# The expert stage of a two-block transformer kernel on one core: weights stored by pairs of experts, TensorE's order written out, the loop for overfull experts after the first pair

## The chip, the core and the metric

The kernel runs on one core of one Trainium2 chip. The metric is the device time of one execution in microseconds (us), lower is better. A core has four compute engines that matter here: TensorE (PE in the profile; its weight loads are listed apart as PEld), VectorE (DVE), ScalarE (ACT) and GpSimd (POOL), and SyncE (SP), which issues most of the transfers from memory. [...]

## What is computed

The reference runs a first block (a mixer of differential attention and an mLSTM, cross-attention, a mixture of experts) and then two layers of a second block. All tensors are float32, 512 tokens of 1024 features. The change touches the mixture of experts alone. There are 32 experts of 512 hidden features in 4 groups; each token goes to two of them:

```
def hierarchical_moe(h, w_rg, b_rg, w_re, b_re, w1, w3, w2):
    ...
    top_p, top_i = lax.top_k(jax.nn.softmax(e_logits, axis=-1), TOP_K)
    comb = g_w[:, None] * top_p / jnp.sum(top_p, axis=-1, keepdims=True)
    ...
    def run_block(args):
        x_blk, e = args
        return (jax.nn.silu(x_blk @ w1[e]) * (x_blk @ w3[e])) @ w2[e]
    ...
    out = jnp.zeros((n_tok + 1, d), yb.dtype).at[buf_tok].add(yb)[:n_tok]
    return out.reshape(bsz, seq, d)
```

Every expert's weights are read once: w1 and w3 are 1024 x 512, w2 is 512 x 1024, together 6 MiB per expert and 192 MiB for all.

## The kernel before

**Slots and pairs.** The routing step finds a place for every token in its two experts. An expert has 64 slots (`SLOT`); two experts, `2 * pr` and `2 * pr + 1`, form a pair and share the 128 rows of a tile, so there are 16 pairs. For a pair the stage does the following, each a step by name in `plan` and a function in `experts`:

- `sel`: VectorE makes one-hots `Sel` of tokens by slots.
- `gather`: TensorE multiplies the tokens' rows (in two float16 halves, `hh` and `hl`) by `Sel`, 32 products for each half of the features (`gs`), into a bank named `tr`; VectorE copies the result with a gain to `xg`.
- `w13`: the rows `xg` times w1 and w3, into two banks `h`. The products are float32 and only 64 columns of the array wide, one for each expert of the pair: expert 0 writes the partitions 0 to 63 of a bank, expert 1 the partitions 64 to 127 (`pair`). A float32 product shows as two records in the trace.
- `marks`: four transposes of `Sel` and four small products; ScalarE copies the turned one-hots to `sT`, VectorE reduces the slots' weights to `cw`.
- `hidden`: ScalarE takes a tanh of bank `h`, two VectorE steps make silu(h1) * h3 in `hm`.
- `turn`: four transposes of `hm` into a `tr` bank, ScalarE copies to `hT`.
- `w2` and `y`: `hT` times w2 into two banks `y`, in halves of the output's columns; ScalarE and VectorE split the result into `yh` and `yl`.
- `combine`: for each of 4 tiles of tokens and each half of the columns two products of `sT` with `yh` and `yl` into a `tr` bank, which VectorE adds to `x`. There are two `tr` banks, and `gather`, `marks`, `turn` and `combine` all take turns on them.

**Order.** `plan` sets the order in which the steps are written: `w13` of pair p in four pieces, with `turn`, `w2`, `y` and `combine` of pair p - 1 and the `gather` of pair p + 1 between them. The framework's scheduler then orders each engine's instructions by their dependences and priorities, so TensorE's order need not be the written one.

**Weights.** A piece is 1 MiB, 128 partitions of 2048 float32, and belongs to one expert: four pieces hold w1 and w3, two hold w2. A step of `w13` takes two pieces, one of each expert. There are 19 slots for pieces (`RINGS`); `fetch` writes the loads on SP's queue in the order of use, `piece` writes those up to 15 ahead of the piece that is taken. A load waits on SP until the slot's last user on TensorE is done, and what stands behind it on the queue waits too.

**Overfull experts.** `more` is a loop that runs as often as there are blocks of tokens past the 64 slots. Its count comes from the data; with these inputs the trace has no instruction of its body. Every engine passes the loop's head and they wait for each other there. It stands in pair 4 (`MORE`).

Of the kernel before, what the change touches and what calls it, by code (L numbers as in the profile page):

```python
# [32 lines left out]
MORE = 4  # L33
# [25 lines left out]
def brow(ap):  # L59
    """A row of memory for all partitions."""  # L60
    return bass.AP(tensor=ap.tensor, offset=ap.offset, ap=[[0, P], [1, ap.shape[-1]]])


class Kern:
    def __init__(self, ctx, tc, a):
        self.ctx, self.tc, self.nc, self.a = ctx, tc, tc.nc, a
        self.ssq = {}

    # ---------------------------------------------------------------- pools
# [36 lines left out]
    def split(self, src, hi, lo, scale, ahead=None):  # L106
        """hi + lo = src * scale, each in float16."""
# [6 lines left out]
    def raw_w(self, src, n=2048):  # L114
        """One piece of weights from memory."""
# [4 lines left out]
    def load_w(self, src, n=2048, raw=None):  # L120
        """A piece of weights, split in two halves, by parts of 1024 columns."""
# [11 lines left out]
    def chunk(self, w, c, width):  # L133
        """Chunk c of a piece in halves, a number of columns wide."""
# [3 lines left out]
    def rstd4(self, pool, ss, n, scale):  # L138
        """(ss * scale + EPS) ** -0.5 of a compact [128, n] tile."""
# [7 lines left out]
    def rstd_row(self, pool, src, tag="junk"):  # L147
        """(mean of squares + EPS) ** -0.5 of rows of D, a half at a time."""
# [10 lines left out]
    def bcast_rows(self, pool, r, n, tag):  # L159
        """Row t of every partition = r[t], for n tiles of tokens: [128, n * 128]."""  # L160
# [17 lines left out]
    def grow(self, pool, name):  # L178
        """A gain by features, for all partitions."""
# [4 lines left out]
    def norm_T(self, pool, src, g, xh, xl, i, bank="tr"):  # L184
        """The normalised rows of tile i, by features, in halves."""
# [16 lines left out]
    def raw_steps(self, pool, x, g, xh, xl, r4, i, hf):  # L202
        """A half of the rows of tile i by the gain, by features, in halves; the norm's factor beside it."""
# [8 lines left out]
    def half_rstd(self, pool, x, r4, i, hf, m):  # L212
        """r4[:, i] = m * (mean of squares + EPS) ** -0.5 of the rows, by halves."""
# [10 lines left out]
    def turn_split(self, t, xh, xl, bank="tr", scale=SA):  # L224
        """Four blocks of features of a tile of tokens, turned, in halves."""
# [5 lines left out]
    def consts(self, low):  # L231
# [5 lines left out]
        # the functions' tables are in by the time the rows are  # L237
# [29 lines left out]
    def silu_c(self, pool):  # L267
        """The second block's condition, through its silu, by features, to memory."""
# [8 lines left out]
    def late_consts(self):  # L277
# [3 lines left out]
        # key after query: rows are queries in the one, keys in the other  # L281
# [27 lines left out]
    # ---------------------------------------------------------- first mixer  # L309
    def mixer(self, low, big, pool, early, adp):  # L310
# [28 lines left out]
        # queries and keys of the differential attention, turned  # L339
# [66 lines left out]
    def proj_feat(self, w, xs, width, b, n=S, m=P, out=None, cs=range(DC)):  # L406
        """Columns b*128.. of a piece [d, width] by tokens: [128 features, n tokens]."""
# [8 lines left out]
    def proj_tok(self, w, xs, i, width=256, out=None):  # L416
        """Tokens of tile i by the columns of a piece: [128 tokens, width]."""
# [6 lines left out]
    def turned_head(self, y, yy, c):  # L424
        """One block of features of all tokens, turned, with its gain, in halves."""
# [94 lines left out]
            # root mean square over the head's values  # L520
# [12 lines left out]
    def mlstm(self, pool, xh, xl, qh, ql, gateb, yy):  # L533
# [4 lines left out]
        # gates: logarithms of the forget gates summed up, in rows of tokens  # L538
# [27 lines left out]
        # exp(-m) * SA  # L566
# [3 lines left out]
        # queries and keys: convolution over the tokens, silu  # L570
# [19 lines left out]
        # values with a column of ones, output gates  # L590
# [18 lines left out]
        for h in range(4):  # L609
# [43 lines left out]
            # layer norm over the head  # L653
# [1237 lines left out]
```

## Time and profile before

| | us |
|---|---|
| median of 3 executions | 1729.56 |
| lowest, highest | 1729.55, 1733.49 |
| span of the profiled execution, first to last instruction | 1725.9 |
| expert stage, first to last product with w1 or w3 | 506.2 to 1049.9 |
| tanh of the first pair to tanh of the last (15 pairs) | 522.47 to 1049.66 |

The profile was taken of one execution, for which only the span is listed; the median of the runs is 3.7 us more, which is what lies ahead of the first and behind the last instruction. [...] A DMA share of 1.00 means that all 16 of the core's DMA engines were busy in the stretch. In a row of TensorE's timeline the first number is the start and the second the duration to the end of the last record of the row; the distance between the starts of two rows is the time that TensorE spent on the first, since products are pipelined.

### The profile page before, as it was taken

To read this page: it belongs to the slowest core of one execution; us is meant where nothing else is said; L and a number is where in the kernel's file an instruction comes from. 1 tells how busy PE (TensorE), PEld (TensorE's weight loads), DVE (VectorE), ACT (ScalarE), POOL (GpSimd) and SP (SyncE) were. 2 spreads that over 40 slices of the span, in tenths; PEclk is the share of its full clock that TensorE was granted. 3 is DMA by queue.
4 is the path that set the end of the run, shared out by engine and by line. 5 is a ranking of instruction groups with operands and counts; after the bars stand their busy time and mean duration, and the time that the engine had idled before them with its cause. 6 is when DMAs were issued, how large, how long until landed. Compare 5 with 4: busy or idle time off the path is not lost.

```text
span 1725.9 us, 25286 instructions
## 1 busy us (share of the span) xinstructions
PE 1583.1 (92%) x10208; PEld 832.1 (48%) x10208; DVE 975.8 (57%) x2076; ACT 592.2 (34%) x1230; POOL 113.1 (7%) x124
## 2 busy tenths in 40 slices
PE   7999998989989999999999997798899989888998
PEld 5344676855763333333333332533444674334457
DVE  5779758877562222322232225789465657866462
ACT  5255455323420100011000103732466545227461
POOL 0210001000000000000000002301100012010000
PEclk9999999999999999999999999999999999989999
DMA  7410233995849987999887852133211222340201
GB/s 275 154 53 25 98 111 99 346 293 182 311 183 420 398 328 291 427 399 386 353 339 309 329 220 98 56 99 89 88 49 50 87 68 74 101 125 25 73 26 50
DMA packets 55609, 323.03 MB, mean 187 GB/s; under 512 B 8720, under 2 KB 11584, under 8 KB 19520
## 3 DMA queue, kind: packets, MB, share of 16 engines
q1 hardware_dynamic: 45136, 306.01, 46.8%
q10 hardware_dynamic: 10352, 15.37, 3.4%
q8 instruction: 81, 1.33, 0.3%
q14 instruction: 40, 0.33, 0.1%
HBM read 310.35 MB, written 3.69 MB: 182 GB/s over the span
## 4 chain that ended last, share of the span: by engine, by line
PE 41%; DVE 10%; DMA 4%; ACT 3%; issue 2%; POOL 1%; ACTq 0%; DVEq 0%; POOLq 0%; SPq 0%
PE h L98 10%; PE mm L98 6%; PE cv L98 6%; PE y L98 5%; PE tr L98 5%; PE po L98 4%; PE at L98 3%; DMA R<-cu 3%; DVE sc L1573 1%; DVE m L1572 1%; PE tr L1614 1%; DVE wl L112 1%; DVE sc L1568 1%; DVE yl L112 1%; POOL rs_r L144 1%
## 5 line engine op out<-in xcount | busy, mean ns | idle before, releaser
L98 PE MATMUL h<-raw,xg 128*64 128x512 f32 x1024 | 307.4, 604 | 0.0
L112 DVE SCALAR_TENSOR_TENSOR wl<-raw,wh 128x1024 f16<-128x1024 f32 (+1 forms) x107 | 135.5, 1271 | 63.2 <-ACT wh L111 63.1
L98 PEld LDWEIGHTS <-wh 128*128 128x128 f16 x1104 | 107.5, 100 | 123.4 <-issue 32.3
L98 PEld LDWEIGHTS h<-raw,xg 128*64 128x64 f32 x1024 | 82.4, 137 | 147.1 <-issue 138.8
L98 PE MATMUL y<-raw,hT 128*64 128x512 f32 x512 | 143.7, 595 | 0.7 <-ACT hT L961 0.7
L111 ACT ACTIVATE wh<-raw 128x1024 f16<-128x1024 f32 (+1 forms) x107 | 110.6, 1042 | 91.6 <-PE mm L98 41.8
L112 DVE SCALAR_TENSOR_TENSOR yl<-y,cw,yh 128x512 f16<-128x512 f32 x32 | 24.0, 751 | 190.2 <-ACT yh L111 183.1
L979 DVE SCALAR_TENSOR_TENSOR x<-tr,x 128x512 f32<-128x512 f32 x128 | 84.4, 687 | 46.6 <-PE tr L98 45.4
L111 ACT ACTIVATE yh<-y,cw 128x512 f16<-128x512 f32 x32 | 22.0, 687 | 246.5 <-PE y L98 246.5
L98 PEld LDWEIGHTS <-hh 128*128 128x128 f16 x768 | 73.9, 100 | 35.3 <-issue 30.4
L98 PEld LDWEIGHTS <-wl 128*128 128x128 f16 x552 | 54.9, 100 | 64.0 <-issue 14.5
L98 PEld LDWEIGHTS y<-raw,hT 128*64 128x64 f32 x512 | 42.7, 136 | 69.7 <-issue 67.1
L98 PE MATMUL po<-R,wd 128*32 128x512 f16 x768 | 55.6, 394 | 21.9 <-DMA R<-cu 21.9
L98 PE MATMUL cv<-hl,wh 128*128 128x512 f16 x192 | 74.9, 390 | 0.0
L98 PE MATMUL cv<-hh,wl 128*128 128x512 f16 x192 | 74.9, 390 | 0.0
L98 PE MATMUL cv<-hh,wh 128*128 128x512 f16 x192 | 74.7, 389 | 0.0
L98 PEld LDWEIGHTS <-hl 128*128 128x128 f16 x640 | 64.0, 100 | 4.6 <-issue 2.1
L919 DVE TENSOR_TENSOR xg<-tr,gcol 128x512 f32<-128x512 f32 x30 | 20.7, 692 | 79.5 <-PE tr L98 79.5
L935 ACT ACTIVATE sT<-tr 128x512 f16<-128x512 f16 x16 | 9.6, 597 | 163.2 <-PE tr L933 157.4
L1230 DVE CUSTOM_DVE_ANT_0 raw<-raw,cact 128x1024 f32<-128x1024 f32 x48 | 58.3, 1238 | 10.9 <-DMA raw<-in_w_ada 9.5
L98 PEld LDWEIGHTS <-sT 128*128 128x128 f16 x256 | 20.2, 97 | 89.0 <-issue 75.1
L98 PE MATMUL tr<-yh,sT 128*128 128x512 f16 x128 | 48.8, 384 | 14.6 <-DVE x L979 8.0
(429 smaller groups left out, 3521.3 us busy)
## 6 DMA issues: line engine op xcount, KB each, us to landing
raw<-in_w_moe SPq DMA_DIRECT2D x192, 1024.0 KB, 7.9
raw<-in_w_pre SPq DMA_DIRECT2D x34, 1024.0 KB, 5.7
raw<-in_w_big SPq DMA_DIRECT2D x30, 1024.0 KB, 4.9
raw<-in_w_ada SPq DMA_DIRECT2D x24, 1024.0 KB, 5.2
R<-cu ACTq DMA_DIRECT2D x32, 271.0 KB, 5.0
x<-in_x_tm SPq DMA_DIRECT2D x4, 512.0 KB, 7.3
gt<-in_r ACTq DMA_DIRECT2D x4, 512.0 KB, 5.4
out<-x SPq DMA_DIRECT2D x4, 512.0 KB, 2.6
```

The source lines that it names most:

```text
L98: self.last_mm = self.nc.tensor.matmul(out, lhsT, rhs, start=start, stop=stop, skip_group_check=True)
L111: return (nc.scalar.activation(hi, src, func, scale=scale), nc.vector.scalar_tensor_tensor(lo, src, scale, hi, op0=OP.mult, op1=OP.subtract))
L112: nc.vector.scalar_tensor_tensor(lo, src, scale, hi, op0=OP.mult, op1=OP.subtract))
L144: self.last_pow = nc.gpsimd.tensor_tensor(r[:, :n], t[:, :n], self.mhalf[:, :n], OP.pow)
L919: self.nc.vector.tensor_tensor(xg, pv, self.gcol[:, 4 * g:4 * g + 4, None].to_broadcast([P, 4, P]), OP.mult)
L935: nc.scalar.activation(sT, pt, AF.Copy)
L979: self.last_add = nc.vector.scalar_tensor_tensor(xo, pc, 1.0 / 1024.0, xo, op0=OP.mult, op1=OP.add)
L1230: nc.vector.tensor_tensor_reduce(w, w, cact, 1.0, 0.0, OP.mult, OP.add, to)
L1568: nc.vector.scalar_tensor_tensor(sc, re[:, :W], s, sc, op0=OP.mult, op1=OP.add)
L1572: nc.vector.max(m8, sc)
L1573: nc.vector.match_replace(sc, m8, sc, -3.0e38)
L1614: nc.tensor.transpose(pt[:, (i - k) * P:(i - k + 1) * P], ps_[i][:, k * P:(k + 1) * P], self.ident)
```

## The change

The weights are laid out anew in memory, outside the measured kernel: a piece is still 1 MiB but holds the same part of both experts of a pair. So `w13` of a pair is eight pieces, one for each 128 features, and `w2` is four. `piece` writes loads up to 18 ahead in place of 15.

`plan` writes another order. All of `w13` of a pair comes first, then `hidden` and `marks`, then eight units, each with eight products of the gather of the next pair (`rows`) and one `combine` of the pair before; `turn` stands after the sixth unit (`TURNED`), and `w2` of the same pair follows the units. While the stage is written, `pinned` is set, and every product and transpose goes through `pin`, which has the scheduler keep TensorE's instructions in the written order. The other engines are still ordered by the scheduler.

The gather gets two banks of its own, `ga`; of the four banks `h` two are left. `more` moves behind `w13` of the first pair, ahead of its `hidden`, and uses the banks `y` and `ga`.

```diff
-MORE = 4
+TURNED = 5
...
+        self.pinned = False
...
-        self.last_mm = self.nc.tensor.matmul(out, lhsT, rhs, start=start, stop=stop, skip_group_check=True)
+        self.last_mm = self.pin(self.nc.tensor.matmul(out, lhsT, rhs, start=start, stop=stop, skip_group_check=True))
         return self.last_mm
+    def turned(self, out, src, ident):
+        return self.pin(self.nc.tensor.transpose(out, src, ident))
+    def pin(self, ins):
+        return self.tc.keep_in_program_order(ins) if self.pinned else ins
...
         for p in range(n):
-            was, more = p > 0, p + 1 < n
-            steps += [("w13", p, 0), ("marks", p)]
...
+            more = p + 1 < n
+            if p:
+                steps += [("sel", p + 1)] * more
+            steps += [("w13", p, c) for c in range(DC)]
+            if p == 0:
+                steps += [("more",), ("sel", 1)]
+            steps += [("hidden", p), ("marks", p)]
+            units = [(i, f) for i in range(NT) for f in range(2)]
             if more:
+                steps.append(("open", p + 1))
+            for u, (i, f) in enumerate(units):
+                if more:
+                    steps.append(("rows", p + 1, i, f))
+                if p:
+                    steps.append(("combine", i, (f,)))
+                if u == TURNED:
+                    steps.append(("turn", p))
+            if more:
+                steps += [("close", p + 1)]
+                for k in range(2):
+                    steps += [("w2", p, k, 0), ("w2", p, k, 1), ("y", p, k)]
...
-        self.fetch(k + sum(RINGS) - 4)
+        self.fetch(k + sum(RINGS) - 1)
...
-            raws = [self.piece(2 * pr + j, q).rearrange("p (c f) -> p c f", c=2) for j in range(2)]
-            for cc in range(2):
-                for k in range(2):
-                    for j in range(2):
-                        self.up13(self.ph, k, raws[j][:, cc, k * 512:(k + 1) * 512], xgs[2 * pr + q // 2], 2 * q + cc, pair[j])
+            raw = self.piece(pr, c).rearrange("p (j k f) -> p j k f", j=2, k=2)
+            for k in range(2):
+                for j in range(2):
+                    self.up13(self.ph, k, raw[:, j, k], xgs[2 * pr + c // 4], c, pair[j])
...
+        self.pinned = True
         for st in self.steps:
             do[st[0]](*st[1:])
+        self.pinned = False
...
-            K.banks(c1, "ps2", tr=2, h=4, y=2)
+            K.banks(c1, "ps2", tr=2, ga=2, h=2, y=2)
```

**TensorE, a pair in the stage.** In the names, `h` is a bank of `w13`, `y` one of `w2`, `raw` a piece of weights, `tr<-yh,sT` and `tr<-yl,sT` the two products of a `combine`; the numbers tell tiles apart. Before, in the middle of a pair, with pieces of one expert each:

```order
L98 MATMUL tr_7667<-yl_7579,sT_7319 128x512
L98 MATMUL h_7726<-raw_7432,xg_7615 64x512
L98 MATMUL h_7727<-raw_7430,xg_7615 64x512
L98 LDWEIGHTS sT_7319
L98 MATMUL tr_7671<-yh_7578,sT_7319 128x512
```

Now, at the end of a pair's units, its `w2` and the first `w13` of the next pair:

```order
L99 MATMUL tr_7529<-yl_7339,sT_7204 128x512
L99 MATMUL y_7537<-raw_7165,hT_7507 64x512 x4
L99 MATMUL y_7537<-raw_7171,hT_7507 64x512 x4
L99 MATMUL y_7538<-raw_7177,hT_7507 64x512 x4
L99 MATMUL y_7538<-raw_7183,hT_7507 64x512 x4
L99 MATMUL h_7571<-raw_7189,xg_7533 64x512 x2
L99 MATMUL h_7572<-raw_7189,xg_7533 64x512 x2
```

Where single products with w1 and w3 stood between the products of the combines, all 16 products of `w2` now stand in one run, and the 32 of `w13` in the next, both experts side by side.

**VectorE, a pair in the stage.** `hm` is `hidden`, `cw` belongs to `marks`, `Sel` to `sel`, the steps on `x` are the adds of the combines. Before, where the adds of a pair meet the next `hidden`:

```order
L112 SCALAR_TENSOR_TENSOR yl_8005<-y_7991,cw_7752,yh_8004 128x512
L979 SCALAR_TENSOR_TENSOR x0_82<-tr_8089,x0_82 128x512
L979 SCALAR_TENSOR_TENSOR x1_83<-tr_8093,x1_83 128x512
L950 SCALAR_TENSOR_TENSOR hm_8081<-hm_8081,h_7939 128x512
L979 SCALAR_TENSOR_TENSOR x1_83<-tr_8097,x1_83 128x512
L951 TENSOR_TENSOR hm_8081<-hm_8081,h_7940 128x512
```

Now, from the end of a pair's `w13` on:

```order
L958 SCALAR_TENSOR_TENSOR hm_6769<-hm_6769,h_6719 128x512
L1074 TENSOR_REDUCE cw_6785<-tr_6780 64x1
L959 TENSOR_TENSOR hm_6769<-hm_6769,h_6720 128x512
L1074 TENSOR_REDUCE cw_6785<-tr_6780 64x1
L1062 TENSOR_TENSOR Sel_6930<-slots_4687,pos_5161 128x512
L1075 TENSOR_SCALAR cw_6785<-cw_6785 128x1
L987 SCALAR_TENSOR_TENSOR x0_82<-tr_6799,x0_82 128x512
```

`hidden`, the reductions and the one-hots of a later pair now all stand ahead of the first add of a pair.

**SP, the loads around the loop.** `raw<-in_w_moe` is the load of a piece, `TENSOR_LOAD n_more` and the branch are the loop's head. Before:

```order
L1036 DMA raw<-in_w_moe 128x2048 x66
L1139 TENSOR_LOAD n_more
L1143 COMPARE_AND_BRANCH
L1143 UNCONDITIONAL_BRANCH x2
L1886 BRANCH_PREFETCH_HINT
```

Now:

```order
L1043 DMA raw<-in_w_moe 128x2048 x21
L1153 TENSOR_LOAD n_more
L1157 COMPARE_AND_BRANCH
L1157 UNCONDITIONAL_BRANCH x2
L1908 BRANCH_PREFETCH_HINT
```

Four loads stand further ahead in both; so 25 of the 192 pieces are now issued before the loop's head, where 70 were. Ahead of the stage and behind it the order of every engine is what it was.

## Rows read from the trace of the kernel before

**Rows 1.** The page: its span, and the chain that ended last by engine.

```profile
span 1725.9 us, 25286 instructions
...
PE 41%; DVE 10%; DMA 4%; ACT 3%; issue 2%; POOL 1%; ACTq 0%; DVEq 0%; POOLq 0%; SPq 0%
```

**Rows 2.** Tile h: one record's ns min/median/max, first and last start in us.

```profile
L98 PE MATMUL h<-raw,xg x1024: 592/592/1116, 506.2 to 1049.9; 128*64 128x512 f32 x171
```

**Rows 3.** ACT's timeline (start, us, what): one tanh for each pair, five of 16.

```profile
691.52 0.60 ACT L949 ACTIVATE hm<-h 128x512 f32<-128x512 f32 x1 [1.86 <-PE h L98]
723.69 0.60 ACT L949 ACTIVATE hm<-h 128x512 f32<-128x512 f32 x1 [1.86 <-PE h L98]
...
976.87 0.60 ACT L949 ACTIVATE hm<-h 128x512 f32<-128x512 f32 x1 [5.13 <-PE h L98]
1014.84 0.60 ACT L949 ACTIVATE hm<-h 128x512 f32<-128x512 f32 x1 [5.13 <-PE h L98]
1049.66 0.60 ACT L949 ACTIVATE hm<-h 128x512 f32<-128x512 f32 x1 [5.13 <-PE h L98]
```

**Rows 4.** Windows of one pair: us, busy by engine, PEclk, DMA share, GB/s.

```profile
764.15:796.30 32.15, 32.15 (x190) 12.25 (x190) 10.49 (x18) 3.17 (x5) 0.00 (x0) 1.00 0.97 391
...
908.10:946.10 38.00, 35.75 (x190) 13.56 (x190) 10.30 (x18) 3.17 (x5) 0.00 (x0) 1.00 0.86 332
```

**Rows 5.** PE's timeline in a pair of 32 us, 736 to 759 us.

```profile
736.68 0.64 PE L958 MATMUL tr<-ident,hm 128*128 128x128 f32 x4
...
744.26 0.23 PE L98 MATMUL tr<-Sel,hh 128*128 128x128 f16 x1
...
746.15 3.65 PE L98 MATMUL h<-raw,xg 128*64 128x512 f32 x16
749.64 3.60 PE L98 MATMUL y<-raw,hT 128*64 128x512 f32 x16
753.07 3.60 PE L98 MATMUL h<-raw,xg 128*64 128x512 f32 x16
756.61 0.39 PE L98 MATMUL tr<-yh,sT 128*128 128x512 f16 x1
...
757.58 1.07 PE L98 MATMUL h<-raw,xg 128*64 128x512 f32 x2
758.58 0.39 PE L98 MATMUL tr<-yh,sT 128*128 128x512 f16 x1
```

**Rows 6.** PE's timeline in a pair of 38 us, 895 to 898 us.

```profile
895.85 0.38 PE L98 MATMUL tr<-yh,sT 128*128 128x512 f16 x1 [0.72 <-ACT yh L111]
...
897.79 0.38 PE L98 MATMUL tr<-yh,sT 128*128 128x512 f16 x1 [0.35 <-DVE x L979]
```

**Rows 7.** All engines' timeline, last pair: a combine, its adds, the start of w2.

```profile
1045.37 0.38 PE L98 MATMUL tr<-yl,sT 128*128 128x512 f16 x1 [0.41 <-DVE yl L112]
...
1045.79 1.29 DVE L979 SCALAR_TENSOR_TENSOR x<-tr,x 128x512 f32<-128x512 f32 x2 [0.47 <-PE tr L98]
...
1046.53 0.38 PE L98 MATMUL tr<-yh,sT 128*128 128x512 f16 x1 [0.35 <-DVE x L979]
...
1055.61 3.65 PE L98 MATMUL y<-raw,hT 128*64 128x512 f32 x16 [0.75 <-ACT hT L961]
```

**Rows 8.** DVE's timeline around the loop's head.

```profile
659.24 3.44 DVE L979 SCALAR_TENSOR_TENSOR x<-tr,x 128x512 f32<-128x512 f32 x5 [3.77 <-PE tr L98]
664.10 0.69 DVE L1055 TENSOR_TENSOR Sel<-slots,pos 128x512 f16<-128x512 f32 x1 [1.42 <-ACT hm L949]
```

**Rows 9.** SP's timeline ahead of the stage: loads of pieces, counted at the end.

```profile
443.54 24.05 SPq L1036 DMA_DIRECT2D raw<-in_w_moe  x10
...
495.68 6.55 SPq L1036 DMA_DIRECT2D raw<-in_w_moe  x5
```

**Rows 10.** Windows: the early stage; and four us behind the loop's head.

```profile
540.00:560.00 20.00, 20.00 (x111) 7.14 (x108) 7.72 (x13) 1.28 (x2) 0.00 (x0) 1.00 1.01 427
...
664.00:668.00 4.00, 4.00 (x36) 3.21 (x36) 2.67 (x4) 0.00 (x0) 0.00 (x0) 0.57 0.89 303
```

More of the change, by code (lines that the diff above doesn't have):

```diff
@@ L986, in plan @@
         steps = [("blocks",)]
-        w2 = lambda p, k: [("w2", p, k, 0), ("w2", p, k, 1), ("y", p, k)]
         for p in range(n):
-            was, more = p > 0, p + 1 < n
-            steps += [("w13", p, 0), ("marks", p)]
-            if more:
-                steps.append(("sel", p + 1))
-            if was:
-                steps.append(("turn", p - 1))
-            steps.append(("w13", p, 1))
-            if was:
-                steps += w2(p - 1, 0)
-            if more:
-                steps.append(("gather", p + 1, (0,)))
-            steps.append(("w13", p, 2))
-            if was:
-                steps += w2(p - 1, 1)
-            steps.append(("w13", p, 3))
-            if p != MORE:
-                steps.append(("hidden", p))
-            if was:
-                steps += [("combine", i, (0, 1)) for i in range(NT)]
-            if p == MORE:
-                steps += [("more",), ("hidden", p)]
-            if more:
-                steps.append(("gather", p + 1, (1,)))
@@ L1013, in plan @@
+        steps += [*w2(0)[:2], ("latent", 0), ("y", n - 1, 0),
                   *[("combine", i, (0,)) for i in range(NT)], ("sums",), ("latent", 1),
-                  *w2(n - 1, 1), *[("combine", i, (1,)) for i in range(NT)]]
+                  *w2(1), *[("combine", i, (1,)) for i in range(NT)]]
         self.steps, self.order = steps, []
@@ L1017, in plan @@
             if st[0] == "w13":
-                self.order += [(2 * st[1] + j, st[2]) for j in range(2)]
-            if st[0] == "w2" and st[3] == 0:
-                self.order += [(2 * st[1] + j, 4 + st[2]) for j in range(2)]
+                self.order.append((st[1], st[2]))
+            if st[0] == "w2":
+                self.order.append((st[1], DC + 2 * st[2] + st[3]))
         self.order[-2:-2] = [(NE, 0), (NE, 1)]
@@ L1033, in fetch @@
             raw = self.rings[k % sum(RINGS)].tile([P, 2048], F32, name="raw", tag="raw")
[L1034 to L1036 removed]
+            pr, q = self.order[k]
+            if pr < NE:
+                self.nc.sync.dma_start(raw, self.a["w_moe"][pr, q])
             else:
@@ L1100, in w2 @@
         def w2(pr, k, half):
-            if half == 0:
-                if k == 0:
-                    self.py = [self.bank("y"), self.bank("y")]
-                self.raws = [self.piece(2 * pr + j, 4 + k).rearrange("p (f o) -> p f o", f=4) for j in range(2)]
-            for f in (2 * half, 2 * half + 1):
+            if k == half == 0:
+                self.py = [self.bank("y"), self.bank("y")]
+            raw = self.piece(pr, DC + 2 * k + half).rearrange("p (j f o) -> p j f o", j=2, f=2)
+            for f in range(2):
+                g = 2 * half + f
                 for j in range(2):
-                    self.mm(self.py[k][pair[j]], hT[pr][:, f, pair[j]], self.raws[j][:, f], f == 0, f == 3)
+                    self.mm(self.py[k][pair[j]], hT[pr][:, g, pair[j]], raw[:, j, f], g == 0, g == 3)
         def y(pr, k):
@@ L1128, in sums @@
                                           accum_out=self.fss[:, i:i + 1])
-        do = dict(sel=sel, gather=gather, marks=mark, w13=w13, hidden=hidden, turn=turn, w2=w2, y=y,
+        do = dict(sel=sel, open=rows_open, rows=rows, close=rows_close, marks=mark, w13=w13, hidden=hidden, turn=turn, w2=w2, y=y,
                   combine=lambda i, f: self.combine(quad[-1], i, halves=f), more=lambda: self.more(pool, moe),
                   blocks=lambda: self.blocks(pool), latent=latent, sums=sums)
+        self.pinned = True
         for st in self.steps:
             do[st[0]](*st[1:])
+        self.pinned = False
     def more(self, pool, moe):
```

57 lines of the change are left out of this document (32 added, 25 removed).

## The prediction

> **What bounds the kernel now.** I read the page first: of the chain that ended last TensorE holds 41% [rows 1]. The only stage that the change touches runs from the first product with w1 or w3 at 506.2 to the start of the last at 1049.9 us [rows 2], which I end at 1050.3; that is 544 of 1725.9 us. Then I asked for the tanh of each pair, since one per pair gives the period [rows 3]. There are two periods: 32.17 us (691.52 to 723.69) and 37.97 us (976.87 to 1014.84). The windows of one pair say what sets them [rows 4]. [...] So TensorE's own sequence is the bound in both, and the stream follows it. A pair is 12.58 MB, which over 32.17 us is the 391 GB/s of the first window: that is TensorE's pace and not the stream's limit, which shows where slots are free: 427 GB/s at a DMA share of 1.01 [rows 10].
>
> The timeline of TensorE shows what the sequence loses. Eight products of w1, w3 or w2 in one run (16 records) take 3.43 to 3.49 us, 0.43 each [rows 5], because the two experts' products run side by side on the two halves of the array. A product that stands alone between combines (two records at 757.58) holds TensorE for 1.00 us until the next starts [rows 5]: its partner is missing, and there is a switch to float16 products (about 0.14: 1.00 less two records at 0.43). In the long pairs there are waits besides, as 0.72 us for `yh` and 0.35 us for an add [rows 6].
>
> **The change, a full pair.** TensorE's work in the new order, each kind by its count and a row [rows 5]: 32 products of w13 at 0.43 are 13.8; 16 of w2, 6.9; the 64 of the gather, two lots of 32 in 1.89 us (744.26 to 746.15), 3.8; the 16 of the combines, four lots of four in 0.97 us (756.61 to 757.58), 3.9; the turn 0.6; marks, eight small records that no row above shows alone, between nothing and the turn's 0.6, and I take 0.6, the nearest row. Together 29.6. The lots of 1.89 and 0.97 hold a switch each, six in all, where the new order switches three times a pair: less 3 x 0.14, so 29.2.
>
> To that come the waits of a fixed order, since TensorE can no longer do something else when a bank is late. Let E be the end of w13. The tanh starts 0.6 us before E [rows 2, 3] and takes 0.60; then ScalarE copies `sT`, of the same size, so until about E + 1.1. VectorE does the two steps of `hidden` and the one-hots, three steps of one size at the 0.69 of the one-hots [rows 8], with the small reductions between, before its first add at about E + 2.5. TensorE wants the bank of `sT` for the first combine at E + 1.1 (marks 0.6, eight products of the gather 0.5), that of the reductions for the second at E + 2.1, and the first add's bank for the third at E + 3.0, where the add (0.65, half of a row of two) ends at 3.15 [rows 7]. From there a unit of TensorE is 0.95 us against an add of 0.65, so TensorE sets the pace. I price this at 0.5 us a pair; it can be 0, and the upper end is the rival below. **Period: 29.7 us.** The other queues have cover: the load of a piece is issued when its slot is free, up to 18 pieces ahead; with two banks `h` in place of four the next w13 comes some 15 us after `hidden` has read them; `w2` waits for `hT`, whose copy runs beside the last two units; `close` (two copies of about 0.69) runs beside w2's 6.9 us. Where one of these covers failed, it would cost its own 0.6 to 1.4 us a pair.
>
> **The first pair and the loop.** w13 runs for 13.8 us. Then all engines meet at the loop. Before, VectorE's last add ended at 662.68 (659.24 + 3.44) and its next step began 1.42 us later [rows 8]. I take 1.4 here, with nothing to wait for but w13's end. Behind it comes `sel`, 0.69, now beside marks; then the gather 3.8, turn 0.6, w2 6.9: 27.2 us in all. On SP only loads stand behind the loop. Piece 25 is the first of them, its slot is the seventh piece's, and TensorE frees that about 2 us before the loop, so the stream has loads in flight across it. A granted clock of 0.57 for some 4 us stood behind the loop before [rows 10], and may again; up to 1.7 us, left to the range.
>
> **The sum.** The last w13 ends at 506.2 + 27.2 + 14 x 29.7 + 13.8 = 963.0, against 1050.3: 87.3 us earlier. The last pair then pays: its eight combines of the pair before now stand behind w13 with no gather between, so VectorE sets it: two steps of `hidden` 1.4, eight adds at 0.65 are 5.2, a copy 0.6, so w2 starts 7.2 us after E, where it started 5.3 us after (1055.61) [rows 7]: 1.9 us lost, between 0 and 3. Behind that the order is unchanged. Span 1725.9 - 85.4 = 1640.5; the median lies 3.7 above the span (1729.56), so **1644 us**.
>
> **Does the stream keep up?** Fifteen loads are issued ahead of the stage [rows 9] after four earlier ones, so all 19 slots are on their way when the first product runs. The first slot comes free at about 508, and 169 more pieces of 1.05 MB are needed up to the end of the last w13. With some 5 us for landing and use, at 427 GB/s (2.46 us a piece) that ends at 928, well before 963; at 391 (2.68) at 966. It decides below about 394 GB/s.
>
> **Rivals.**
> *The stream sets the pace.* If 391 GB/s is its sustained limit after all (its DMA share was 0.97 [rows 4]), the last w13 ends at 966 and the time is 1647. If it were held at the 332 GB/s of the long pairs [rows 4] (3.16 us a piece, 1047) nothing would be gained: 1728. Midway between the two windows, at 361 (2.90 us a piece, 1003), it would be 1684. Against all of it: 427 was reached where slots were free [rows 10], and these two rates are those of TensorE's pace.
> [...]
>
> *Banks one at a time.* If each combine waited for the add of the one before, a combine would take 1.38 us (0.22 for its first product, then 1045.37 to 1046.53) [rows 7], the gather hidden in the wait: 11.0 us for eight in place of 7.7, a period of 33.1, and 1692. For it: turn, marks and combines share two banks. Against: two banks alternate, and the gather's 0.47 lies between.
>
> [...]
>
> That the order is not kept is no rival: the built kernel has it.
>
> **How the numbers follow.** The forecast, TensorE's sequence at 29.7 us: 0.70, 1644 us. The stream at 391: 0.10, 1647. At 361: 0.02, 1684. Banks one at a time: 0.09, 1692. A stream that gains nothing: 0.04, 1728. The clock: 0.05, 1752. For the range: no waits at all (14 x 0.5), no loss at the end and marks at 0.3 bring 1644 down to about 1632; waits of 1.9 us a pair, the clock behind the loop and the stream at 391 bring it to 1670. These two ends leave out the last four cases, 0.20. Faster by over 0.3% (about what a measurement of this kernel can tell from no change): 0.91. Within it: 0.04. Slower: 0.05.
>
> **What would show it.** Right: tanh to tanh 29 to 31 us for fourteen pairs, all alike; w13 as one run of 64 records in 13.8 us; the stream at some 424 GB/s over a pair (12.58 MB in 29.7 us) with no wait of TensorE for a piece; the last product with w1 or w3 near 963. Wrong: TensorE's waits on `raw` (the stream), waits of 0.7 us or more at each combine (banks), a granted clock under 1.00 in the middle of pairs (clock), or a second block that runs longer than before.

## The result and the profile after

The changed kernel takes 1646.86 us (median of 5 runs, 1645.52 to 1654.38), against 1730.62 (5 runs, 1729.55 to 1733.49): a ratio of 0.953, 95% interval 0.951 to 0.955. The forecast was 1644 us, within 1632 to 1670. The sum of the prediction came out 3 us off, but two of its terms missed by more than that, in opposite directions: the loop cost 10.0 us where 1.4 were taken, and each pair took 0.44 us less than forecast, 6.2 us over fourteen.

From the page of the changed kernel, the counterpart of [rows 1]: the span, engine times, and in 40 slices the clock granted to TensorE (a share of full speed, here in tenths) and the stream.

```profile
span 1652.7 us, 25283 instructions
PE 1511.4 (91%) x10208; PEld 828.4 (50%) x10208; DVE 973.2 (59%) x2076; ACT 592.0 (36%) x1230; POOL 113.7 (7%) x124
PEclk9999899999998999999999998989999999989999
GB/s 284 157 62 12 91 82 111 290 255 328 147 224 283 385 426 427 427 426 427 426 426 426 426 154 14 109 105 131 10 68 43 75 96 100 67 121 26 77 26 52
PE 48%; DVE 9%; DMA 3%; ACT 3%; issue 2%; POOL 1%; ACTq 0%; DVEq 0%; POOLq 0%
```

The profiled execution is the slowest of the five. The expert stage begins 5.3 us later in it than before (511.47 against 506.2), although nothing changed ahead of it; in the other profiled executions of this study it begins between 505.35 and 513.48. So times are compared below from the first product with w1 or w3 to the last tanh: 543.5 us before (506.2 to 1049.7), 459.7 after (511.47 to 971.14). That is 83.8 us, the whole difference of the medians. Within this stretch the first run of w13 products takes 14.5 to 16.0 us from one profile to another, since the granted clock is still low at its start (0.58 to 0.79 between 505 and 512 us in four profiles), so a difference of about a microsecond there says nothing.

The tanh of the pairs, the counterpart of [rows 3]: start, duration, what, and in brackets ScalarE's idle time ahead and what ended it.

```profile
534.65 0.60 ACT L957 ACTIVATE hm<-h 128x512 f32<-128x512 f32 x1 [24.38 <-SPq L1157]
561.70 0.60 ACT L957 ACTIVATE hm<-h 128x512 f32<-128x512 f32 x1 [12.19 <-PE h L99]
590.96 0.60 ACT L957 ACTIVATE hm<-h 128x512 f32<-128x512 f32 x1 [12.19 <-PE h L99]
620.22 0.60 ACT L957 ACTIVATE hm<-h 128x512 f32<-128x512 f32 x1 [12.19 <-PE h L99]
649.47 0.60 ACT L957 ACTIVATE hm<-h 128x512 f32<-128x512 f32 x1 [12.19 <-PE h L99]
...
942.07 0.60 ACT L957 ACTIVATE hm<-h 128x512 f32<-128x512 f32 x1 [12.19 <-PE h L99]
971.14 0.60 ACT L957 ACTIVATE hm<-h 128x512 f32<-128x512 f32 x1 [12.19 <-PE h L99]
```

Where [rows 3] had two periods, 32.17 and 37.97, there is one of 29.26 us, every pair alike to 0.02 and the last 0.2 shorter. Only the first row is of another kind: its tanh waited for SyncE at line 1157, the loop.

One full pair, from its tanh to the next: the window (engine busy times with counts, granted clock, DMA share, GB/s), and TensorE's timeline without the gather's products.

```profile
620.22:649.48 29.26, 29.09 (x190) 12.65 (x188) 10.37 (x18) 3.17 (x6) 0.00 (x0) 1.00 1.01 426
```

```profile
620.96 0.40 PE L103 MATMUL tr<-identh,Sel 128*128 128x128 f16 x4
621.19 0.24 PE L99 MATMUL tr<-chl,Sel 128*128 128x4 f16 x4
622.04 0.38 PE L99 MATMUL tr<-yh,sT 128*128 128x512 f16 x1
622.26 0.38 PE L99 MATMUL tr<-yl,sT 128*128 128x512 f16 x1
...
627.12 0.65 PE L103 MATMUL tr<-ident,hm 128*128 128x128 f32 x4
...
629.47 7.09 PE L99 MATMUL y<-raw,hT 128*64 128x512 f32 x32
636.38 13.90 PE L99 MATMUL h<-raw,xg 128*64 128x512 f32 x64
```

TensorE is busy for 29.09 of 29.26 us at a granted clock of 1.00. The 64 records of w1 and w3 are one run of 13.90, those of w2 one of 7.09; everything else lies in the 8.51 us between (620.96 to 629.47). Of all the waits of TensorE in a pair one is left that is worth naming, first row below: the turn waits 0.4 us for VectorE's add to free its bank, once a pair. The second row is all that TensorE waited for pieces of weights between 540 and 950 us (what waited, what for, us in all, times, longest).

```profile
PEld tr L103 <- DVE x L987: 5.6, 14, 0.4
PEld y L99 <- DMA raw<-in_w_moe: 0.4, 1, 0.4
```

### The profile page after: what moved, and what is told of

Its sections match the earlier page's. It is cut to its first block, busy times and chain, and to the rows that moved or that the text cites. A ratio compares the mean times of both kernels' runs of the same rounds, so it can differ in the third digit from the quotient of the medians.

```text
span 1652.7 us, 25283 instructions
## 1 busy us (share of the span) xinstructions
PE 1511.4 (91%) x10208; PEld 828.4 (50%) x10208; DVE 973.2 (59%) x2076; ACT 592.0 (36%) x1230; POOL 113.7 (7%) x124
## 3 DMA queue, kind: packets, MB, share of 16 engines
q8 instruction: 81, 1.33, 0.3%
## 4 chain that ended last, share of the span: by engine, by line
PE 48%; DVE 9%; DMA 3%; ACT 3%; issue 2%; POOL 1%; ACTq 0%; DVEq 0%; POOLq 0%
PE h L99 12%; PE y L99 6%; PE mm L99 6%; PE cv L99 6%; PE po L99 4%; PE tr L99 4%; PE at L99 3%; PE ga L99 3%; DMA R<-cu 3%; DVE sc L1593 1%; DVE m L1592 1%; PE tr L1634 1%; DVE wl L120 1%; PE tr L103 1%; DVE sc L1588 1%
## 5 line engine op out<-in xcount | busy, mean ns | idle before, releaser
L99 PE MATMUL h<-raw,xg 128*64 128x512 f32 x1024 | 223.0, 593 | 0.0
L99 PEld LDWEIGHTS h<-raw,xg 128*64 128x64 f32 x1024 | 73.5, 137 | 146.1 <-issue 145.7
L958 DVE SCALAR_TENSOR_TENSOR hm<-hm,h 128x512 f32<-128x512 f32 x16 | 11.0, 687 | 180.5 <-ACT hm L957 180.5
L99 PE MATMUL y<-raw,hT 128*64 128x512 f32 x512 | 113.6, 595 | 0.0
L957 ACT ACTIVATE hm<-h 128x512 f32<-128x512 f32 x16 | 9.6, 597 | 207.2 <-PE h L99 182.8
L99 PEld LDWEIGHTS y<-raw,hT 128*64 128x64 f32 x512 | 35.3, 137 | 70.3 <-issue 69.0
L99 PE MATMUL ga<-Sel,hl 128*128 128x128 f16 x480 | 67.8, 223 | 0.0
L99 PE MATMUL ga<-Sel,hh 128*128 128x128 f16 x480 | 67.8, 223 | 0.0
## 6 DMA issues: line engine op xcount, KB each, us to landing
raw<-in_w_moe SPq DMA_DIRECT2D x192, 1024.0 KB, 12.1
```

Of the source, the lines that this page charges most:

```text
L99: self.last_mm = self.pin(self.nc.tensor.matmul(out, lhsT, rhs, start=start, stop=stop, skip_group_check=True))
L957: nc.scalar.activation(hm[:n], ph[0][:n], AF.Tanh, scale=0.5 / SA)
L958: nc.vector.scalar_tensor_tensor(hm[:n], hm[:n], 1.0, ph[0][:n], op0=OP.add, op1=OP.mult)
```

## The hole at the loop

TensorE's first run of w1 and w3 ended at 525.93. Then it stood for nine microseconds. Two sets of rows lead to the cause: what TensorE waited for, and what SyncE's queue waited for at the loop's head, in the changed kernel (500 to 560 us).

```profile
PE tr L103 <- SPq L1157: 9.0, 1, 9.0
```

```profile
SPq L1157 <- SPq L1157: 10.3, 3, 5.3
```

In the kernel before (640 to 670 us) the same queue showed this:

```profile
SPq L1143 <- DVEq L1139: 8.5, 1, 8.5
...
SPq L1143 <- SPq L1143: 3.8, 1, 3.8
```

SyncE issues all loads of weights. At the head of this loop it waits, one semaphore after another, until the loads that it issued earlier have landed: in the changed kernel these waits ended at 528.98, 531.44 and 533.91, 2.46 us apart, which is the time of a piece at 427 GB/s; the trace has landings at 531.43 and 533.89. Before, SyncE did the same (3.8 us, to 653.41, with a landing at 653.39), but it came to the loop some 13 us ahead of TensorE and VectorE (at 649 us, they at 662), and then waited 8.5 us for VectorE; the landing was hidden.

There is a second suspect in the same place, the sequencer's own branches at the loop (duration min/median/max in ns, first and last start in us), first of the changed kernel, then of the one before.

```profile
L1157 PEldq COMPARE_BRANCH  x3: 97/193/6201, 522.2 to 534.7; - x3
```

```profile
L1143 PEldq COMPARE_BRANCH  x3: 101/187/310, 662.1 to 663.6; - x3
```

One branch of TensorE, the jump over the loop's body, took 6.20 us, from 526.14 to 532.34; before, 0.31. So there were two theories. **A**: SyncE's wait for the loads in flight makes the hole. **B**: TensorE's branch does. And there was the forecast's own reading, a fixed 1.4 us and something else wrong with the first pair.

**The yardstick and the loop's price.** The changed kernel once more, and without the loop:

```diff
-                steps += [("more",), ("sel", 1)]
+                steps += [("sel", 1)]
```

> The changed kernel itself, as the yardstick for the runs beside it. Profiled before: 1646.9 us median, the first pair's tanh 8.7 us behind the end of its w13 products (525.93 to 534.65), a period of 29.26 us from the second pair on. Both theories of the hole at the loop (the engines wait there until the weights' loads already issued have landed; or TensorE's own branch, recorded at 6.20 us, holds it) expect the same again: 1647 us, hole 8.7 us. If the hole were an accident of one execution it would be near the 1.4 us that the prediction took.

> Leaves out the loop for overfull experts (its body runs zero times with these inputs, so that the output stays the same here; with other inputs tokens would be missing). Prices the loop. If the hole of 9.0 us on TensorE (525.93 to 534.95) is the loop's and the granted clock of 0.52 behind it (535 to 540, some 2.4 us lost) follows from the hole: 9.0 + 2.4 = 11.4 us less, 1635.5 us, and the first pair's tanh 0.6 us ahead of the end of its w13 products as in every other pair. If the loop costs the 1.4 us of the prediction and the hole has another cause (the first pair's pieces arrive late), 1645.5 us and the hole stays.

Measured: 1647.74 us (ratio 0.952, 0.950 to 0.955) and 1636.25 (0.946, 0.943 to 0.948). From the first w13 product to the last tanh the two took 459.8 and 449.8 us. The first pair, from its first product to that of the second pair, took 37.28 (505.49 to 542.77) and 27.24 us (506.57 to 533.81). The loop costs 10.0 us, and not 1.4. It is not only the hole. The granted clock behind it in the changed kernel (columns as above):

```profile
526.00:535.00 9.00, 0.05 (x1) 0.06 (x2) 0.20 (x1) 0.35 (x1) 0.00 (x0) 0.70 0.62 258
535.00:540.00 5.00, 5.00 (x52) 5.00 (x53) 2.73 (x7) 0.84 (x2) 0.00 (x0) 0.52 0.63 218
540.00:546.00 6.00, 6.00 (x48) 3.06 (x47) 1.29 (x2) 1.21 (x2) 0.00 (x0) 1.00 0.63 223
```

After 9 us without work TensorE ran for 5 us at 0.52 of full clock, and in the six after them at 1.00. In the kernel without the loop the same stretch has 1.00 throughout.

**Fewer loads ahead of the loop.** The loads that w13 of the first pair would issue are held back and issued behind the loop, so that 22 or 19 stand ahead of it on SyncE's queue in place of 25 (`cap` is `sum(RINGS) + 3` or `sum(RINGS)`).

```diff
-        self.fetch(k + sum(RINGS) - 1)
+        self.fetch(min(k + sum(RINGS) - 1, self.cap))
...
-                steps += [("more",), ("sel", 1)]
+                steps += [("more",), ("refill",), ("sel", 1)]
...
+        def refill():
+            self.cap = len(self.order)
+            self.fetch(self.taken + sum(RINGS) - 2)
```

> The last three loads that stand ahead of the loop on SP's queue (the 23rd to the 25th piece) are put behind it; nothing else is moved. Theory A, the loop's head waits for the landing of every load issued before it: in the changed kernel SP's waits there ended at 528.98, 531.44 and 533.91, 2.46 us apart as pieces land, so the 22nd lands at about 526.5 and TensorE goes on at about 527.5 in place of 534.95: 7.4 us less, 1639.5 us, or 1637 if the granted clock then stays up. Theory B, TensorE's own branch, 6.20 us from 526.14, holds it whatever is in flight: it goes on at 532.5, 2.5 us less, 1644.5 us. If neither counts: 1647.

> All six loads that w13 of the first pair issues ahead of the loop are put behind it, so that 19 stand ahead. Theory A: the 19th lands at about 519, before w13 ends at 525.9, so the hole is as short as with 22 (about 1.5 us): 1639.5 us, or 1637 with the clock up. The stream then stands some 10 us in place of 4; with 11 pieces landed ahead of TensorE this is hidden, and if it isn't, waits of TensorE on pieces give up to 6 us back (1645). Theory B: TensorE's branch takes 6.20 us again, 1644.5 us; if that branch is slow because the loads in flight hold up what it fetches, it shrinks here more than with 22, where the loads end only 0.4 us behind its start.

Measured: 1647.42 us (0.951, 0.948 to 0.953) and 1642.88 (0.950, 0.948 to 0.952). The whole time scatters by as much as the effect; the stretch from the first w13 product to the last tanh does not: 456.2 and 456.0 us, 3.6 and 3.8 less than the yardstick. So neither theory is right alone. A held for the other engines: with 22 loads SyncE was through its landings 0.8 us after w13's end and ScalarE's tanh followed at once; with 19 all was landed before. But TensorE went on only 4.7 us after w13's end in both. These are its wait and its branch with 19 loads ahead, and the DMA traffic meanwhile (523.5 to 527.7 us: queue, kind, packets, MB, share):

```profile
PE tr L103 <- issue: 4.7, 1, 4.7
```

```profile
L1161 PEldq COMPARE_BRANCH  x3: 97/192/3321, 519.6 to 527.7; - x3
```

```profile
q1 hardware_dynamic: 105, 0.86, 62.0%
q8 instruction: 1, 0.02, 1.4%
q14 instruction: 1, 0.01, 1.1%
```

The branch shrank from 6.20 to 3.32 us with no load in flight ahead of it. It is 3.32 or 3.33 us in the three profiles with 22 or 19 loads ahead and this place of the loop, and 5.8 to 6.2 in those with nothing held back. Inside it lies one packet on queue 8, whose kind is "instruction". The page counts 81 such packets with 1.33 MB, 16 KB each, over the whole kernel. That is one for every 252 of TensorE's 20,416 recorded instructions; in the trace of the changed kernel TensorE begins 254 between one and the next at the median, and a kernel with 256 instructions fewer (the one with less work for TensorE, below) shows 80 packets. From these counts I take the packets for TensorE's program on its way to the engine; that is an estimate. With 19 loads ahead the packet runs between 524 and 525 us, about 1 us after the branch begins; in the changed kernel, with loads in flight, from 529.90 to 530.93, 3.8 us after. Queue 14 carries instructions too, in packets of 8 KB, but none of its packets lies inside the branch of 6.20 us. In the kernel before no packet of queue 8 lay inside the branch or in the 12 us ahead of it.

**The place of the loop in TensorE's program.** Does it matter where in TensorE's program the branch stands? To find out, every instruction of TensorE was moved by a few places: with 19 loads ahead, 16 tiny products that nobody reads were put at TensorE's very start, where it waits 10 us for the first rows. If the place decides, I expected a branch of 0.2 to 0.4 us with no such packet inside it, some 453 us from the first w13 product to the last tanh, and 1640 us.

```diff
         nc.scalar.activation(self.fss, self.mhalf[:, :NT], AF.Square)
+        ahead = self.bank("ax")
+        for i in range(16):
+            self.mm(ahead[:16, :16], self.mhalf, self.mhalf, True, True)
```

> The kernel with 19 loads ahead of the loop, and 16 tiny products (16x16 on a zeroless constant, their result is never read) put at TensorE's very beginning, where it waits 10 us for the first rows anyway. They do no work; they only move every later instruction of TensorE some 32 to 64 places on. With 19 loads ahead TensorE's branch at the loop still took 3.32 us, with a fetch of 16 KB of TensorE's instructions inside it; in the kernel before the same branch took 0.31 us, and there the last such fetch lay 13 us ahead of it. [...] Rival (a jump with nothing else in flight costs 3.3 us whatever its place): the same as without the products, 456.0 and 1643 us.

Measured: 1642.12 us (0.949, 0.947 to 0.951), and 451.6 us from the first w13 product to the last tanh, 8.2 less than the yardstick. TensorE's branch, the wait that is left, and the clock behind it:

```profile
L1164 PEldq COMPARE_BRANCH  x3: 97/187/310, 521.2 to 526.3; - x3
```

```profile
PE tr L103 <- DVE hm L961: 1.7, 1, 1.7
```

```profile
525.00:530.00 5.00, 3.45 (x60) 3.45 (x61) 2.97 (x7) 1.19 (x2) 0.00 (x0) 1.00 0.71 233
530.00:535.00 5.00, 5.00 (x38) 2.32 (x37) 1.29 (x2) 0.90 (x2) 0.00 (x0) 1.00 1.02 424
```

The branch is back at 0.31 us, with no packet of queue 8 between 516 and 525.4 us, the hole is 1.7 us (the prediction took 1.4 for it), and the granted clock stays at 1.00. The loads issued late cost nothing visible: the period stays 29.26. So the hole had two causes in one place: loads in flight that must land (A), and TensorE's jump over the body (a form of B), which was slow where a packet of queue 8 lay inside it. While 25 loads stood ahead the first hid the second: the branch ended at 532.34, and the last landing came at 533.89. No run has the 25 loads with a fast jump, but by these times its hole would be as long. The tiny products moved the branch by 64 places in TensorE's program (32 records of products and 32 weight loads), so these runs show that the place decides, 0.31 us against 3.32; the run on the last pair, below, has them too and shows 0.31 us again. With loads in flight the slow place took 6.20. Why one place is slow and the other is not was not shown, nor that the packet is the cause.

This version is better than the changed kernel by 8.2 us in the stage. Of the whole time 5.6 us show against the yardstick, with intervals that just overlap (0.947 to 0.951 against 0.950 to 0.955), since the executions scatter by some 8 us ahead of the stage.

**The fetch depth.** The depth of the kernel before, alone:

```diff
-        self.fetch(k + sum(RINGS) - 1)
+        self.fetch(k + sum(RINGS) - 4)
```

> Undoes the fetch depth alone: a load is issued 15 pieces ahead of the piece in use, as in the kernel before, in place of 18. In the first pair this puts 22 loads ahead of the loop in place of 25. Theory (the deeper fetch brings nothing in the pairs, where TensorE sets the pace, and costs something at the loop, where the loads issued before it must land): period 29.26 us, no waits of TensorE for pieces, and from the first w13 product to the last tanh about 456 us as with the 22 loads of the other run, against 459.8: 1643 us. Rival (at 427 GB/s the stream needs every slot, so three pieces less in flight leave it short): waits for pieces and a period of 29.5 us or more, 1650 or more.

Measured: 1645.05 us (0.951, 0.948 to 0.954), the period 29.26, no wait of TensorE for a piece between 560 and 940 us, and 456.3 us from the first w13 product to the last tanh, as with the 22 loads. The deeper fetch of the change brings nothing in the pairs and costs 3.5 us at the loop.

## What makes a pair 29.26 us

**The pin and the written order.** One kernel has the new order, pieces and banks without the pin; one is the kernel before with the pin, in its old order.

```diff
-        self.pinned = True
+        self.pinned = False
         for st in self.steps:
```

> Only the pin is taken away: the written order, the pieces by pairs and the banks stay, and the scheduler may move TensorE's work. In the built order most pairs stay as written; from some of the middle pairs on, single products with w1 and w3 come between the combines, as before. Theory (the written order brings the gain, the pin only guards it): pairs left as written keep 29.26 us, and a pair with four lone groups of products pays some 0.14 to 0.3 us for each switch and now and then a wait, so 30 to 31 us: in all 1650 to 1665. Rival (the pin itself is what matters, since without it waits of up to 0.7 us come back at each lone product): periods of 32 us or more from there on, 1675 or more.

```diff
-        self.last_mm = self.nc.tensor.matmul(out, lhsT, rhs, start=start, stop=stop, skip_group_check=True)
+        self.last_mm = self.pin(self.nc.tensor.matmul(out, lhsT, rhs, start=start, stop=stop, skip_group_check=True))
...
+    def pin(self, ins):
+        return self.tc.keep_in_program_order(ins) if self.pinned else ins
```

> The kernel before with one thing added: TensorE keeps the order in which its old plan is written (pieces of one expert, four h banks, gathers in two halves, eight combines in one run, the loop in the fifth pair all stay). Theory (the new written order is what makes TensorE nearly free of waits; the pin only keeps it): the old order has eight combines in a run against VectorE's 0.65 us each and two steps of hidden ahead of them, 6.6 us against TensorE's 3.6, so some 3 us of waits a pair and twice as many switches: a period near 33 us, against 34.0 on average before: 1710 to 1720. Rival (the pin is the whole gain, whatever the order): a period near 29.3 in the pairs, 1650 to 1660.

Measured: without the pin 1696.41 us (0.982, 0.978 to 0.985), the old order with it 1689.04 (0.975, 0.972 to 0.977). Neither half brings the gain, and both theories missed: 1650 to 1665 was forecast for the first, 1710 to 1720 for the second. Without the pin four intervals between tanhs, from the second on, are 29.2 us; from where the scheduler moves products the intervals are 32.3, 37.5 and then 34.4 for six pairs. One of the 34.4, by its window and by TensorE's timeline (in brackets the idle time and what ended it):

```profile
816.94:851.34 34.40, 31.22 (x190) 11.97 (x188) 10.59 (x18) 3.05 (x5) 0.00 (x0) 1.00 0.98 368
```

```profile
818.91 0.22 PE L99 MATMUL ga<-Sel,hh 128*128 128x128 f16 x1 [1.16 <-DVE xg L927]
...
825.72 1.94 PE L99 MATMUL y<-raw,hT 128*64 128x512 f32 x8
827.59 0.39 PE L99 MATMUL tr<-yh,sT 128*128 128x512 f16 x1
...
831.52 0.59 PE L99 MATMUL tr<-yh,sT 128*128 128x512 f16 x2 [0.79 <-ACT yh L119]
831.95 0.38 PE L99 MATMUL tr<-yl,sT 128*128 128x512 f16 x1
832.26 1.94 PE L99 MATMUL h<-raw,xg 128*64 128x512 f32 x8
...
842.67 0.22 PE L99 MATMUL ga<-Sel,hh 128*128 128x128 f16 x1 [0.79 <-DVE xg L927]
```

Busy time is 31.22 in place of 29.09, which I put down to more switches between kinds of products, and three microseconds are waits of 0.4 to 1.2 us for VectorE and ScalarE, which stand where the written order has other work. I had priced the switches and only now and then a wait (30 to 31 us); the rival's 32 or more was right. With the old order pinned the period is 32.30 us in eleven of fifteen intervals, TensorE busy for 29.64 of 31.50 us (700 to 731.5); the forecast of 33 was near, but I had set it against a mean of 34.0 before, where the mean interval from tanh to tanh was 35.1 (527.2 / 15). That is the two periods of [rows 3]: with the pin the old order stays near the shorter one, 32.17, in pairs that took 37.97 without it. The new order takes the period from 32.30 on to 29.26. So the stage took 495.3 us with the pin alone, 504.4 with order, pieces and banks alone, 459.7 with both, against 543.5 before. No run changes the banks alone.

**The pieces.** The new order with the old pieces, one expert each, taken two at a time:

```diff
-            raw = self.piece(pr, c).rearrange("p (j k f) -> p j k f", j=2, k=2)
+            if c % 2 == 0:
+                self.r13 = [self.piece(pr, c + j).rearrange("p (c k f) -> p c k f", c=2, k=2) for j in range(2)]
```

> Undoes the layout of the pieces alone: a piece again holds one expert (two chunks of w1 and w3, or half of w2), taken two at a time, in the new fixed order. Theory (the layout is worth nothing by itself, since TensorE waited only 0.4 us in all for pieces between 540 and 950 us and the stream has a lead of a dozen pieces): period 29.26 us, 1647 us within 3. Rival (with the stream at 427 GB/s, just about what TensorE takes, pieces freed two at a time break the stream and TensorE waits for pieces): a period of 29.6 us or more, 1652 or more.

Measured: 1648.89 us (0.955, 0.953 to 0.958), a period of 29.26 from the third pair on. The layout by pairs is worth at most the 2 us by which the stage is longer here (461.8 against 459.8), all of it in the first pair, around the loop (39.2 us in place of 37.3).

**TensorE or the stream.** A pair's 12.58 MB in 29.26 us are 430 GB/s, and the stream delivers 426: which of the two sets the pace? One kernel takes work from TensorE, the other bytes from the stream.

```diff
-            self.mm(pc, lhs, yh[:n, o], True, False)
-            self.mm(pc, lhs, yl[:n, o], False, True)
+            self.mm(pc, lhs, yh[:n, o], True, True)
```

> Leaves out the product with the low halves in each combine (eight float16 products a pair, some 0.24 us each; the result loses precision). It asks what bounds a pair now. Theory (the stream is the next bound and already level with TensorE: 12.58 MB at 427 GB/s take 29.5 us): the period falls from 29.26 by nothing or almost nothing once the pieces that landed ahead are used up, TensorE waits for pieces, and the time stays at 1640 to 1648. Rival (TensorE alone sets the pace and the stream has room): period 27.3 us, 14 x 1.9 = 27 us less, 1620 us.

```diff
-                self.order.append((st[1], DC + 2 * st[2] + st[3]))
+                if not st[3]:
+                    self.order.append((st[1], DC + 2 * st[2]))
```

> Leaves out two of the twelve pieces of a pair (the second piece of each half of w2; the first is used twice, so the result is wrong), so 10.49 MB a pair, which take 24.6 us at 427 GB/s. TensorE's work is unchanged. Theory (TensorE's sequence sets the 29.26 us): the period stays 29.26, the stream falls to some 358 GB/s, 1647 us. Rival (the stream sets it): the period falls towards what TensorE needs without waits, below 29.26, and the time below 1640.

Measured, in one execution each: 1629.96 and 1649.74 us. Their windows from 700 to 800 us, first with less work for TensorE, then with fewer bytes:

```profile
700.00:800.00 100.00, 98.10 (x644) 42.87 (x644) 37.05 (x66) 11.47 (x18) 0.00 (x0) 1.00 1.01 426
```

```profile
700.00:800.00 100.00, 99.31 (x674) 44.83 (x672) 39.93 (x70) 11.29 (x18) 0.00 (x0) 1.00 0.92 365
```

With fewer bytes the period is 29.26 again while the stream falls to 365 GB/s: TensorE sets it. With less work it falls to 27.97, and TensorE takes 450 GB/s (12.58 MB in 27.97 us) from a stream that still brings 426. Its waits for pieces come to 3.4 us between 560 and 950 us, twelve of at most 0.3, as much as with fewer bytes. My theory that the stream would bind at once fell: what landed ahead pays for the difference, by my estimate some 1.5 us a pair (29.5 for 12.58 MB at 426 GB/s, less 27.97), and the stage ends before it is used up. The gain of 1.29 us a pair was less than the 1.9 of the rival; TensorE is busy 98.1% there, so part of the rest is waits.

**The last pair.** Its turn and the first two lots of w2 between the eight combines, on top of the tiny products:

```diff
+                if not more and u in (3, 5):
+                    steps.append(("w2", p, 0, u // 5))
-                if u == TURNED:
+                if u == (TURNED if more else 1):
```

> As the run with the tiny products, and the last pair's order changed: the turn behind the second of the eight combines, and the first two lots of w2 behind the fourth and the sixth, so that TensorE has products while VectorE adds. In the changed kernel w2 of the last pair started 7.2 us after the end of the last w13, and ended some 3.4 us later; TensorE's own work up to there is 8.1 us. Theory (VectorE's adds set that stretch): the last of these w2 products ends some 1.5 to 2 us earlier after the last w13, and the time is 1.5 to 2 us below the run beside it, 1638 us. Rival (what follows, the adds and the split of the latent weights on VectorE, sets the end): no gain, 1640 us.

Measured: 1644.31 us (0.948, 0.946 to 0.950), no different from the run beside it (0.949). The first half of w2 ended 1.6 us earlier, 9.9 us after the last tanh in place of 11.5, but the second half of w2 began 16.2 us after it in place of 15.4: the two combines left over and the split of the latent weights then stood in VectorE's way, and the granted clock was 0.72 there (977 to 983 us), against 1.00 in the run beside it (976 to 980). The rival was right.

## Why the prediction was right, and where it was not

- **What bounds it, and the period.** TensorE's own sequence, as said: 29.26 us against 29.7. The runs of w13 (13.8 forecast; 13.84 from its start to that of the next pair's marks at 650.22) and of w2 (6.9) fit. Too large was the stretch between: 9.0 us with waits were taken, 8.51 measured. Marks took 0.34 (eight records from 620.96) in place of the 0.6 borrowed from the turn. The waits of a fixed order were sized right: 0.4 us a pair where 0.5 were taken. But the wait stands at the turn's bank, and not at the first three combines, where the prediction looked for it. Over 14 pairs the period is 6.2 us below the sum.
- **The first pair and the loop.** This is the step that failed, and it is a term mis-sized for want of its mechanism: "I take 1.4 here, with nothing to wait for but w13's end", and of the stream "loads in flight across it". The loop's head let no load fly across it: SyncE's last wait there ended with the last landing, 8.0 us after w13's end. The pair took 37.1 us in place of 27.2 (511.47 to 548.61): the hole 9.0 in place of 1.4, w13 14.5 in place of 13.8 since its granted clock was still low at its start (0.79 between 505 and 512, 0.95 between 512 and 518), and the stretch to the end of w2 13.7 in place of 12.0, for the clock of 0.52 behind the hole. That last was named and left to the range, at up to 1.7 us; it cost more, some 2.4, since the kernel without the loop takes 11.3 us for the same stretch. The rows that could have warned were in the trace: SyncE's waits at line 1143.
- **The end of the stage.** Forecast 7.2 us from the end of w13 to w2, measured 7.2 (971.8 to 979.0), 1.9 us more than before [rows 7]. This row and the step of `hidden` ahead of it:

```profile
971.77 0.69 DVE L958 SCALAR_TENSOR_TENSOR hm<-hm,h 128x512 f32<-128x512 f32 x1 [12.04 <-ACT hm L957]
```

```profile
979.01 3.65 PE L99 MATMUL y<-raw,hT 128*64 128x512 f32 x16
```

- **The sum.** From the first w13 product to the end of the last: forecast 456.8, measured 460.3. The first pair's +9.9 and the pairs' -6.2 nearly cancel, so the median is 2.9 above the forecast. That the total came out right is luck in part: it hid a first pair that was wrong by 10 us. The ends of the range, added up from the prediction's own terms, are some 1631 and 1668 rather than 1632 and 1670.
- **The stream.** 427 GB/s suffices, as forecast; measured 426 from 600 to 900 us and a wait of 0.4 us in all. The two rates held against it, 391 and 332 [rows 4], were TensorE's pace, as said.
- **The rivals.** Banks one at a time do not show, by 0.4 us of waits a pair. No run shows the doubled time of the units in every pair from which the clock's 1752 comes; in its place the granted clock was 1.00 from 620.22 to 649.48 and from 700 to 800 us. It fell outside the pairs' middle, to 0.52 behind the 9 us of the loop.

## What to carry to other kernels

The loop with a count from memory was here a meeting of all engines at which the issuing queue also waited for the loads that it had already issued, 8.0 us beyond TensorE's last product, and TensorE's jump over its body took 3 us more in one place of the program than in another (3.32 against 0.31): where a trace shows this, try holding loads back, and look at how long the sequencers' branches take. An order written out pays in full only if it is kept: here the order (with its pieces and banks) and the pin alone brought 39 and 48 us of stage, both together 84, so the two gains nearly add up. And look past a sum that fits: compare it term by term, by the stage's own rows rather than by the whole time.

## What the runs showed of the hardware

- At this loop's head SyncE's waits ended as its loads landed, 2.46 us apart for pieces of 1 MiB; with 25 and 22 loads ahead the last wait ended 8.0 and 0.8 us after TensorE's last product, and with 19 ahead of it.
- TensorE's jump over the loop's body took 0.31, 3.32 or 6.20 us, by the place of the code (0.31 with the tiny products, 3.32 without) and the loads in flight (6.20 with 25 ahead, 3.32 with 19).
- TensorE's granted clock was 0.50 to 0.57 for 4 to 5 us behind holes of 4.7 and 9.0 us at the loop (with 22 loads ahead still 0.74 in the four after). Behind one of 1.7 us it was 1.00, but behind one of 1.9 us in the kernel before, with several waits of 0.2 to 0.7 us ahead of it, 0.57 [rows 10].
- In the kernel before, two products with w1 and w3 in one run (four records) held TensorE for 1.01 us (759.12 to 760.13), where a lone one of two records held it for 1.00 [rows 5].
- The stream held 426 GB/s from 600 to 900 us, at a median of 12.1 us from issue to landing over the kernel, and TensorE waited for it 0.4 us in all.
